# The decay factors of a long convolution's filters: exponentials on ScalarE instead of 32 loads

## The chip, the core and the metric

The kernel runs on one core of one Trainium2 chip. TensorE (PE) multiplies matrices into an accumulator memory, PSUM, of eight banks; VectorE (DVE) and ScalarE (ACT) work elementwise; GpSimd (POOL) and SyncE (SP) mostly start DMA transfers. Each engine works through its own list of instructions in the order in which they stand, and waits at an instruction until the others have signalled what it needs. The metric is the device time of one execution in microseconds, as the median of several runs.

## What is computed

One block of a diffusion backbone over 1024 latent tokens of width 1024, with 256 context tokens: a modulated norm and one wide input projection; then two token mixers side by side, a neighbourhood attention and a Hyena long convolution; their merge, and a gated feed-forward layer. The change touches the convolution's filters, which depend on no token. For two orders and two directions a small network of the time step gives 512 channels, and each is damped by an exponential decay:

```
t = jnp.linspace(0.0, 1.0, L)[:, None]
hid = jnp.sin(fr * (z @ w1 + b1));  hid = jnp.sin(fr * (hid @ w2 + b2))
h = (hid @ w3).reshape(L, 2, HY_ORDER, HY_WIDTH)
deltas = jnp.abs(jnp.linspace(min_decay, max_decay, HY_WIDTH))
decay = jnp.exp(-t * deltas)
return h * decay[:, None, None, :]
...
k2 = jnp.concatenate([h_fwd, jnp.zeros((1, C)), h_bwd[:0:-1]], axis=0)
y = irfft(rfft(u, n=2 * L) * rfft(k2, n=2 * L))[:L]
```

The decay depends on the time and the channel alone, so it is a constant. The backward filter is used in reversed time, and its first row is zero.

## The kernel before

Tokens or time steps lie on the 128 partitions. Products that need more than one pass of precision are made of three matmuls on a high and a low part of each operand (`split`: ACT casts the high part, `wh` or `oh`; DVE subtracts for the low one, `wl` or `ol`).

Around the change, from about 70 to 300 us, three streams of work are written by Python generators and merged by their planned weights; a scheduler then fixes the order of each engine's list when the program is built:

- `project`, the input projection: a chunk of 128 output columns takes 2 x 24 matmuls of 128x512 (`in_ps`, line 195), chunks of keys and values 24 of 128x256 on the context as well (`ctx_ps`). SP loads the weights (`wr`, line 181), ACT copies results out (`proj`, `projc`), PE turns some of them (`tm_ps`) and ACT copies those (`tm`).
- `filters`, with four groups: two halves `hf` of 256 channels times two orders `o`. I number them 1 to 4 in the order of the program. In a group, four steps of two time blocks each take for both directions `j`: four matmuls into two banks (`filt_ps`, line 363), and two multiplications by the decay tile on DVE (`fv`, line 370), which I call a pair. The decay tiles (`dec`, line 359) are loaded by SP, 128x512 each, from a table that the host computes; `bufs=2` gives them two buffers, so the tile of the next pair may only be loaded when the multiplication of this pair has read its buffer. The matmul results have five banks (`psf`) in common with the stream's other results. Then come DVE's sums and twiddles (lines 376 to 430), whose results `a` are the operands of eight DFTs on PE (`dft_ps`, lines 442 to 444). ACT copies the spectra out (`ks`), and SP writes them to memory (`spec`).
- `ada_rows`, the remaining modulation rows: DVE adds up 64 tiles of a weight (`wal`, loaded by SP into four buffers, line 887) times a column (`aacc`, lines 890 and 892); PE sums over partitions (`ar_ps`) and DVE adds the result (`arow`).

After the filters the same merging goes on with the convolutions, up to about 600 us, and then with attention; the merge and the feed-forward layer follow.

Of the kernel before, what the change touches and what calls it, by code (L numbers as in the profile page):

```python
# [10 lines left out]
F32 = mybir.dt.float32  # L11
F32R = mybir.dt.float32r
AF = mybir.ActivationFunctionType
ALU = mybir.AluOpType
# [4 lines left out]
P = 128  # L19
# [23 lines left out]
def _constants():  # L43

    f32 = np.float32
    out = {}
    n1 = np.arange(P)[:, None].astype(np.float64)
    k1 = np.arange(P)[None, :].astype(np.float64)
    fwd = np.zeros((4, P, 2, 3, P), f32)
    inv = np.zeros((4, P, 2, 3, P), f32)  # L50
    for ci, ks in enumerate(CLASSES):
        for j, kk in enumerate(ks):
            th = TWO_PI * np.mod(n1 * (16 * k1 + kk + 0.5), 2048.0) / 2048.0
            c, s = np.cos(th), np.sin(th)
            if j:
                s = -s
            fwd[ci, :, j, 0], fwd[ci, :, j, 1], fwd[ci, :, j, 2] = c, s, -s
            inv[ci, :, j, 0], inv[ci, :, j, 1], inv[ci, :, j, 2] = c.T, -s.T, s.T
    out["dft_f"], out["dft_i"] = fwd, inv

    L = T
    t = np.linspace(0.0, 1.0, L, dtype=f32)
    w = (f32(TWO_PI) * np.arange(L, dtype=f32)) / f32(L)
    bands = np.linspace(1e-4, 15, 16, dtype=f32)
    bw = bands[None, :] * w[:, None]
    z = np.concatenate([t[:, None], np.cos(bw.astype(np.float64)), np.sin(-bw.astype(np.float64))], 1).astype(f32)
    rev = (L - np.arange(L)) % L
    out["feat"] = np.ascontiguousarray(np.concatenate([z.T, z[rev].T], 0))
    lo, hi = math.log(1e-2) / 1.5, math.log(1e-2) / 0.3
    deltas = np.abs(np.linspace(lo, hi, 512, dtype=f32))  # L70
    dec = np.exp((-t[:, None] * deltas[None, :]).astype(np.float64)).astype(f32) * f32(2.0 ** -10)
    drev = dec[rev].copy()
    drev[0] = 0.0
    both = np.stack([dec, drev], 1).reshape(4, 2, P, 2, 2, 256)
    out["decay"] = np.ascontiguousarray(both.transpose(4, 0, 3, 2, 1, 5)).reshape(2, 4, 2, P, 512)

    tok = np.arange(T)
    rows, cols = (tok // 64).astype(f32), (tok % 64).astype(f32)
    invf = (f32(10000.0) ** (-np.arange(16, dtype=f32) / f32(16))).astype(f32)
    cs, sn = np.zeros((P, T), f32), np.zeros((P, T), f32)  # L80
    for p in range(P):
        d = p % 64
        ang = ((rows if d < 32 else cols) * invf[d % 16]).astype(f32).astype(np.float64)
        cs[p] = np.cos(ang)
        sn[p] = np.sin(ang) * (-1.0 if d % 32 < 16 else 1.0)
    out["rope"] = np.stack([cs, sn])

    return out
# [70 lines left out]
class Block:  # L159
# [43 lines left out]
    def setup(self, pool):  # L203
        nc, a = self.nc, self.a
        self.ident = pool.tile([P, P], F32, name="ident")
        make_identity(nc, self.ident)
        self.eps = pool.tile([P, 1], F32, name="eps")
        nc.vector.memset(self.eps, EPS)
        cc = pool.tile([P, 8, 2], F32, name="cc")
        nc.sync.dma_start(cc, a["cc"])  # L210
        self.cs = pool.tile([P, 48], F32, name="cs")
        nc.vector.memset(self.cs[:, 16:], 0.0)
        nc.scalar.activation(self.cs[:, 0:16], cc.rearrange("p k w -> p (k w)"), AF.Silu)
        self.ng = pool.tile([P, 2, 8], F32, name="ng")
        self.bcol = pool.tile([P, 2, 8], F32, name="bcol")
        self.cw = pool.tile([P, 12, 4], F32, name="cw")
        self.mod1 = pool.tile([P, 2, 2, 8], F32, name="mod1")
        self.mod2 = pool.tile([P, 2, 8], F32, name="mod2")

# [46 lines left out]
    def hidden(self, pool, wpool, mp, hid, w3, hT, hcT, psf):  # L266
        nc, a = self.nc, self.a
        xs = []
        ssq = pool.tile([P, 10], F32, name="ssq1")
        ps = psf.tile([P, 512], F32, tag="f", name="ada_ps")  # L270
# [19 lines left out]

        mlp = self.filter_hidden(mp, hid, psf)
        next(mlp)
        for n in ("ng", "bcol", "cw"):
            nc.scalar.dma_start(getattr(self, n), a[n])
        for k in range(8):
            w = pool.tile([P, 2048], F32, tag="wada", name="wada", bufs=3)
# [51 lines left out]
    def filters(self, pool, psf, hid, w3):  # L348

        nc, a = self.nc, self.a  # L350
        for hf in range(2):
            for o in range(2):
                v = [pool.tile([P, 4, 2, 256], F32, tag="v8", name="fv") for _ in range(2)]
                c0 = o * 512 + hf * 256
                for n2 in range(0, 8, 2):
                    dec, ps = [], []
                    for j in range(2):
                        dec.append(pool.tile([P, 512], F32, tag="dec", name="dec", bufs=2))
                        nc.sync.dma_start(dec[j], a["decay"][hf, n2 // 2, j])
                        ps.append(psf.tile([P, 512], F32, tag="f", name="filt_ps"))  # L360
                    for n in range(2):
                        for j in range(2):
# [4 lines left out]
                                self.tc.keep_in_program_order(mm)  # L367
                    for j in range(2):
                        i = n2 % 4
                        nc.vector.tensor_tensor(v[n2 // 4][:, i:i + 2, j, :], ps[j].rearrange("p (n c) -> p n c", n=2),  # L370
                                                dec[j].rearrange("p (n c) -> p n c", n=2), op=ALU.mult)
                    yield 1.3
                b = pool.tile([1, 256], F32, tag="hb", name="hb", bufs=1)
                nc.sync.dma_start(b, a["hbias"][0:1, o, hf, :])
# [1097 lines left out]
```

## Time and profile before

| what | value |
|---|---|
| runs, median | 1711.23 us (1708.59 to 1711.89, 3 runs) |
| profiled execution, span | 1711.4 us |
| PE busy | 1657.6 us, 97% |
| DVE busy | 1230.1 us, 72% |
| ACT busy | 662.6 us, 39% |
| DMA | 282.48 MB, mean 165 GB/s |
| decay loads | 32 of 256 KB, issued from 75.3 to 274.0 us |

The profile is of one execution. A row of a timeline gives start and length in microseconds, engine, line, operation, output and inputs by the program's names, their shapes, and, in brackets, how long the engine had been idle before and what ended that wait. Runs of like instructions are shown as one row with their number. A row that groups instructions by line gives their number, busy time, mean duration in nanoseconds, and the idle time just before them with its releasers. The "granted clock" is the share of full speed that TensorE's throttle gave.

### The profile page before, as it was taken

The page shows a single profiled execution, that of the slowest core. Times are in us where ns is not written, and L with a number is a line of the kernel's source. Part 1 is how long each engine was busy: PE and PEld are TensorE (multiplying, and loading weights), DVE is VectorE, ACT ScalarE, POOL GpSimd, SP SyncE. Part 2 cuts the span into 40 slices and gives each one's busy share as a digit, 9 for nine tenths or more (in the row PEclk, how much of TensorE's full clock was granted, in tenths as well). Part 3 has the DMA queues.
Part 4 walks back from the last instruction along what each step waited for, and adds up shares of the span by engine and source line. Part 5 has one row for each costly group of instructions (what it writes and reads, how often), then busy time and mean ns, then how long its engine had stood idle before and what let it go on. Part 6 is the DMA issues. An engine that isn't in the chain of part 4 may idle for free.

```text
span 1711.4 us, 22611 instructions
## 1 busy us (share of the span) xinstructions
PE 1657.6 (97%) x8124; PEld 1307.2 (76%) x8124; DVE 1230.1 (72%) x2076; ACT 662.6 (39%) x1141; POOL 153.3 (9%) x274
## 2 busy tenths in 40 slices
PE   6898999999999999999999999999999999999997
PEld 2676776777777778888787888888888888878886
DVE  3697586699995966465865967867865566479576
ACT  4621221312221224455654315733333333355455
POOL 0100211101010014020200000010101011000000
PEclk9999999999999999999999999999999999999999
DMA  9276854645553456344657524333423223395334
GB/s 364 103 255 199 266 173 158 215 139 187 167 201 137 160 187 186 126 148 131 197 174 245 187 65 160 124 124 117 160 99 110 94 99 109 105 383 177 98 120 154
DMA packets 114517, 282.48 MB, mean 165 GB/s; under 512 B 15840, under 2 KB 24676, under 8 KB 112102
## 3 DMA queue, kind: packets, MB, share of 16 engines
q1 hardware_dynamic: 94472, 219.99, 38.6%
q0 software_dynamic: 19280, 60.60, 10.5%
q8 instruction: 64, 1.05, 0.3%
q10 hardware_dynamic: 653, 0.44, 0.1%
q14 instruction: 48, 0.39, 0.1%
HBM read 213.60 MB, written 67.39 MB: 164 GB/s over the span
## 4 chain that ended last, share of the span: by engine, by line
PE 65%; issue 10%; DVE 4%; DMA 2%; ACT 1%; POOL 1%; SPq 0%; DVEq 0%; POOLq 0%; ACTq 0%
PE x_ps L1171 15%; PE in_ps L195 12%; PE z_ps L1171 7%; PE dx_ps L1340 6%; PE out_ps L1109 4%; PE dz_ps L1340 3%; PE hy_ps L195 2%; PE y_ps L1171 2%; PE dft_ps L442 2%; PE pt_ps L800 2%; PE pt_ps L786 2%; PE na_ps L195 2%; PE dy_ps L1340 1%; PE s_ps L766 1%; PE dft_ps L444 1%
## 5 line engine op out<-in xcount | busy, mean ns | idle before, releaser
L195 PE MATMUL in_ps<-hTh,wl 128*128 128x512 f32 x640 | 260.0, 407 | 0.9 <-ACT proj L614 0.5
L195 PE MATMUL in_ps<-hTl,wh 128*128 128x512 f32 x640 | 254.5, 398 | 0.4 <-DVE hTl L176 0.2
L195 PE MATMUL in_ps<-hTh,wh 128*128 128x512 f32 x640 | 253.9, 397 | 0.0
L195 PEld LDWEIGHTS in_ps<-hTh,wl 128*128 128x128 f32 x640 | 121.5, 190 | 32.2 <-issue 5.6
L195 PEld LDWEIGHTS in_ps<-hTl,wh 128*128 128x128 f32 x640 | 121.8, 190 | 27.1 <-DVE hTl L176 1.8
L195 PEld LDWEIGHTS in_ps<-hTh,wh 128*128 128x128 f32 x640 | 121.6, 190 | 26.9 <-issue 0.4
L175 ACT CAST wh<-wr 128x1024 fp32r<-128x1024 f32 (+1 forms) x56 | 51.9, 926 | 141.4 <-PE in_ps L195 110.0
L176 DVE TENSOR_TENSOR wl<-wr,wh 128x1024 fp32r<-128x1024 f32 (+1 forms) x56 | 59.8, 1067 | 63.2 <-ACT wh L175 63.1
L176 DVE TENSOR_TENSOR ol<-ws,oh 128x512 fp32r<-128x512 f32 x88 | 60.4, 688 | 50.6 <-ACT oh L175 50.3
L176 DVE TENSOR_TENSOR ol<-ar,oh 128x512 fp32r<-128x512 f32 x77 | 52.8, 687 | 47.7 <-ACT oh L175 47.7
L175 ACT CAST oh<-ar 128x512 fp32r<-128x512 f32 x77 | 47.9, 622 | 84.4 <-PE dx_ps L1340 33.1
L175 ACT CAST oh<-ws 128x512 fp32r<-128x512 f32 x88 | 54.7, 622 | 57.1 <-PE x_ps L1171 27.5
L442 PE MATMUL dft_ps<-a,matf 128*128 128x512 f32 x128 | 67.1, 606 | 5.0 <-DVE a L430 4.1
L775 ACT ACTIVATE pe<-pe,mx 128x640 f32<-128x640 f32 x64 | 52.6, 822 | 48.9 <-DVE mx L774 48.9
L1340 PE MATMUL dx_ps<-ol,oh 128*128 128x512 f32 x176 | 68.7, 390 | 1.7 <-DVE ol L176 1.7
L774 DVE CUSTOM_DVE_ANT_0 pe<-s_ps,bias 128x640 f32<-128x640 f32 x64 | 50.1, 820 | 28.1 <-PE s_ps L769 28.1
L1340 PE MATMUL dx_ps<-oh,ol 128*128 128x512 f32 x176 | 67.4, 390 | 1.9 <-DVE ol L176 1.9
L1340 PE MATMUL dx_ps<-oh 128*128 128x512 f32 x176 | 68.5, 389 | 0.0
L176 DVE TENSOR_TENSOR ol<-wr,oh 128x512 fp32r<-128x512 f32 x70 | 48.0, 688 | 22.3 <-ACT oh L175 22.2
L175 ACT CAST oh<-wr 128x512 fp32r<-128x512 f32 x70 | 43.3, 622 | 52.3 <-PE x_ps L1171 16.0
L890 DVE SCALAR_TENSOR_TENSOR aacc<-wal,cs,aacc 128x512 f32<-128x512 f32 x56 | 41.8, 747 | 23.1 <-DMA wal<-in_w_ada 22.5
L1111 DVE TENSOR_TENSOR x<-x,out_ps 128x512 f32<-128x512 f32 x64 | 42.6, 683 | 15.2 <-PE out_ps L1109 15.0
(394 smaller groups left out, 4193.7 us busy)
## 6 DMA issues: line engine op xcount, KB each, us to landing
wr<-in_w SPq DMA_DIRECT2D x52, 512.0 KB, 3.4
wr<-in_w_in SPq DMA_DIRECT2D x40, 512.0 KB, 4.2
ar<-g SPq DMA_DIRECT2D x77, 256.0 KB, 2.8
wal<-in_w_ada SPq DMA_DIRECT2D x64, 256.0 KB, 4.1
matf<-in_dft_f SPq DMA_DIRECT2D x32, 384.0 KB, 4.7
bias<-in_rpb SPq DMA_DIRECT2D x64, 192.0 KB, 3.7
g<-t POOLq DMA_DIRECT2D x47, 256.0 KB, 3.0
w<-in_w SPq DMA_DIRECT2D x44, 256.0 KB, 5.4
```

The costliest lines, as they stand in the source:

```text
L175: self.nc.scalar.copy(hi, src)
L176: self.nc.vector.tensor_sub(lo, src, hi.bitcast(F32))
L195: mm = nc.tensor.matmul(ps, ww[:, k * P:(k + 1) * P], xx[:, k, pos:pos + width], start=(i == 0), stop=(i == n - 1))
L442: nc.tensor.matmul(ps, m[:, 0], v.rearrange("p a b -> p (a b)"), start=True, stop=False)
L774: nc.vector.tensor_tensor_reduce(pe, ps[:, 256:896], bt, -1.0, 3e38, ALU.add, ALU.min, mx[:, 0:1])
L775: nc.scalar.activation(pe, pe, AF.Exp, bias=mx[:, 0:1], scale=-1.0, accum_out=mx[:, 1:2])
L786: pin(nc.tensor.transpose(pt[:, at:at + P], pe[:, c * P:(c + 1) * P], self.ident))
L890: nc.vector.scalar_tensor_tensor(acc, w, c, acc, op0=ALU.mult, op1=ALU.add)
L1109: nc.tensor.matmul(ps, gg[x][:, tk], ww[y][:, sl], start=(i == 0), stop=(i == n - 1))
L1111: nc.vector.tensor_add(x1[:, sl], x1[:, sl], ps)
L1171: mm = nc.tensor.matmul(ps, w[u][:, k * P:(k + 1) * P], x[v][:, k, :], start=(start and k == 0 and i == 0), stop=(stop and k == 3 and i == 2),
L1340: nc.tensor.matmul(ps[j], x[u][:, j * P:(j + 1) * P], w[v], start=(start and i == 0 and c == 0), stop=(stop and i == N - 1 and k == len(re ...
```

## The change

The table of decays is gone. The host gives two small arrays instead: `rates`, the decay rate of each channel, and `times`, for each time block and direction the negated time of each partition (with 1000 where the backward filter's first row has to vanish). `times` is loaded once, on ACT's queue, behind three other small loads; `rates` is loaded by SP once for each half, spread over the partitions. Each decay tile is made of two ACT instructions: the exponential of `rates` times the partition's column of `times`. It keeps its two buffers. The factor 2^-10, until now in the table, goes into the multiplication, which becomes an operation with two factors.

```diff
-    dec = np.exp((-t[:, None] * deltas[None, :]).astype(np.float64)).astype(f32) * f32(2.0 ** -10)
...
-    out["decay"] = np.ascontiguousarray(both.transpose(4, 0, 3, 2, 1, 5)).reshape(2, 4, 2, P, 512)
+    tr = t[rev].copy()
+    tr[0] = 1000.0
+    out["rates"] = np.ascontiguousarray(deltas.reshape(2, 1, 256))
+    out["times"] = np.ascontiguousarray(-np.stack([t, tr], -1).reshape(8, P, 2).transpose(1, 0, 2))
...
+        self.times = pool.tile([P, 8, 2], F32, name="times")
...
-        for n in ("ng", "bcol", "cw"):
+        for n in ("ng", "bcol", "cw", "times"):
             nc.scalar.dma_start(getattr(self, n), a[n])
...
         for hf in range(2):
+            rates = pool.tile([P, 256], F32, tag="rates", name="rates", bufs=1)
+            nc.sync.dma_start(rates, a["rates"][hf].broadcast_to((P, 256)))
             for o in range(2):
...
                         dec.append(pool.tile([P, 512], F32, tag="dec", name="dec", bufs=2))
-                        nc.sync.dma_start(dec[j], a["decay"][hf, n2 // 2, j])
+                        for n in range(2):
+                            nc.scalar.activation(dec[j][:, n * 256:(n + 1) * 256], rates, AF.Exp,
+                                                 scale=self.times[:, n2 + n, j:j + 1])
...
-                        nc.vector.tensor_tensor(v[n2 // 4][:, i:i + 2, j, :], ps[j].rearrange("p (n c) -> p n c", n=2),
-                                                dec[j].rearrange("p (n c) -> p n c", n=2), op=ALU.mult)
+                        nc.vector.scalar_tensor_tensor(
+                            v[n2 // 4][:, i:i + 2, j, :], ps[j].rearrange("p (n c) -> p n c", n=2), 2.0 ** -10,
+                            dec[j].rearrange("p (n c) -> p n c", n=2), op0=ALU.mult, op1=ALU.mult)
```

The scheduler sees other work, and so the lists of all engines change between the first filter group and the end of the fourth; from there on they are the same. Line numbers of the changed kernel are a few higher (the exponentials are line 362, the multiplications 374, the DFTs 447 to 449).

ACT's list at group 1, before:

```order
L175 CAST wh<-wr 128x1024
L634 COPY projc<-ctx_ps 128x256
L175 CAST wh<-wr 128x1024
L634 COPY projc<-ctx_ps 128x256
L594 COPY proj<-in_ps 128x512 x2
```

And the same place in the change:

```order
L174 CAST wh<-wr 128x1024
L639 COPY projc<-ctx_ps 128x256
L362 ACT_TABLE_LOAD
L362 ACTIVATE dec<-rates,times 128x256 x10
L174 CAST wh<-wr 128x1024
L362 ACTIVATE dec<-rates,times 128x256 x4
L639 COPY projc<-ctx_ps 128x256
L362 ACTIVATE dec<-rates,times 128x256 x5
L599 COPY proj<-in_ps 128x512
L362 ACTIVATE dec<-rates,times 128x256
L599 COPY proj<-in_ps 128x512
```

Of the group's 16 exponentials, ten stand ahead of the next weight's cast and six behind it; the last four of these twenty belong to group 2's first pair. In group 2, sixteen stand in a row behind the last `ks` copy.

DVE's list at group 2, before (the sums `aacc` of the modulation rows stand between the pairs):

```order
L890 SCALAR_TENSOR_TENSOR aacc<-wal,cs,aacc 128x512 x3
L370 TENSOR_TENSOR fv<-filt_ps,dec 128x2x256 x2
L900 TENSOR_TENSOR arow<-ar_ps,arow 64x256
L375 SCALAR_TENSOR_TENSOR fv<-hb,fv 1x256
L890 SCALAR_TENSOR_TENSOR aacc<-wal,cs,aacc 128x512 x2
L370 TENSOR_TENSOR fv<-filt_ps,dec 128x2x256 x2
L890 SCALAR_TENSOR_TENSOR aacc<-wal,cs,aacc 128x512
L892 TENSOR_SCALAR aacc<-wal,cs 128x512
L890 SCALAR_TENSOR_TENSOR aacc<-wal,cs,aacc 128x512
L370 TENSOR_TENSOR fv<-filt_ps,dec 128x2x256 x2
```

And in the change:

```order
L895 SCALAR_TENSOR_TENSOR aacc<-wal,cs,aacc 128x512 x3
L374 SCALAR_TENSOR_TENSOR fv<-filt_ps,dec 128x2x256 x2
L905 TENSOR_TENSOR arow<-ar_ps,arow 64x256
L380 SCALAR_TENSOR_TENSOR fv<-hb,fv 1x256
L374 SCALAR_TENSOR_TENSOR fv<-filt_ps,dec 128x2x256 x2
L897 TENSOR_SCALAR aacc<-wal,cs 128x512
L374 SCALAR_TENSOR_TENSOR fv<-filt_ps,dec 128x2x256
L895 SCALAR_TENSOR_TENSOR aacc<-wal,cs,aacc 128x512
L374 SCALAR_TENSOR_TENSOR fv<-filt_ps,dec 128x2x256 x2
L895 SCALAR_TENSOR_TENSOR aacc<-wal,cs,aacc 128x512
```

No sum stands between the first and the second pair any more. Behind the group's first two DFT operands, nine sums now stand ahead of the next weight's `wl` and the fifth operand, where four did.

PE's list at group 2, before (the matmuls of the filters among those of the projection):

```order
L363 MATMUL filt_ps<-fw_280,hid 128x256 x4
L897 MATMUL ar_ps<-aacc,ones 32x256 x2
L363 MATMUL filt_ps<-fw_280,hid 128x256 x9
L195 MATMUL in_ps<-hTh,wl 128x512
L195 MATMUL in_ps<-hTl,wh 128x512
L195 MATMUL in_ps<-hTh,wh 128x512
L195 MATMUL in_ps<-hTh,wl 128x512
L363 MATMUL filt_ps<-fw_280,hid 128x256 x3
L195 MATMUL in_ps<-hTl,wh 128x512
```

And in the change:

```order
L367 MATMUL filt_ps<-fw_281,hid 128x256 x4
L902 MATMUL ar_ps<-aacc,ones 32x256 x2
L367 MATMUL filt_ps<-fw_281,hid 128x256 x12
L194 MATMUL in_ps<-hTh,wl 128x512
L194 MATMUL in_ps<-hTl,wh 128x512
```

All sixteen filter matmuls now stand ahead of the projection's. Further on in both lists come 48 (before: 44 more) projection matmuls, 24 of the context, the next `ar_ps`, and then the group's first DFT: behind 37 more projection matmuls before, behind 16 in the change. In group 1 the first DFT stands ten projection matmuls earlier as well.

More of the change, by code (lines that the diff above doesn't have):

```diff
@@ L70, in _constants @@
     deltas = np.abs(np.linspace(lo, hi, 512, dtype=f32))
-    dec = np.exp((-t[:, None] * deltas[None, :]).astype(np.float64)).astype(f32) * f32(2.0 ** -10)
-    drev = dec[rev].copy()
-    drev[0] = 0.0
-    both = np.stack([dec, drev], 1).reshape(4, 2, P, 2, 2, 256)
-    out["decay"] = np.ascontiguousarray(both.transpose(4, 0, 3, 2, 1, 5)).reshape(2, 4, 2, P, 512)
+    tr = t[rev].copy()
+    tr[0] = 1000.0
+    out["rates"] = np.ascontiguousarray(deltas.reshape(2, 1, 256))
+    out["times"] = np.ascontiguousarray(-np.stack([t, tr], -1).reshape(8, P, 2).transpose(1, 0, 2))
     tok = np.arange(T)
```

## The prediction

> **What bounds the kernel now.** I read the page first, then busy time by stretch, then what each engine waited for between 66 and 305 us, where the filters are made, then the timelines of TensorE (PE) and VectorE (DVE) around each stall. Row one is the page's; the others are the view by stretch (length, busy time of PE, PEld, DVE, ACT and POOL, granted clock, DMA share, GB/s).
>
> ```profile
> PE 1657.6 (97%) x8124; PEld 1307.2 (76%) x8124; DVE 1230.1 (72%) x2076; ACT 662.6 (39%) x1141; POOL 153.3 (9%) x274
> 84.00:92.00 8.00, 5.74 (x20) 4.41 (x20) 5.03 (x8) 1.32 (x2) 0.58 (x1) 0.79 0.75 251
> 138.00:150.00 12.00, 7.79 (x22) 5.79 (x23) 5.43 (x9) 0.00 (x0) 0.00 (x0) 0.72 0.84 270
> 231.00:239.00 8.00, 6.07 (x17) 3.67 (x16) 6.81 (x13) 1.10 (x4) 2.56 (x4) 0.79 0.56 181
> 262.00:273.00 11.00, 7.73 (x22) 5.74 (x23) 6.31 (x10) 0.00 (x0) 0.08 (x1) 0.69 0.79 250
> 342.00:428.00 86.00, 85.85 (x358) 64.19 (x358) 83.11 (x146) 18.70 (x27) 6.55 (x9) 1.00 0.50 162
> 428.00:514.00 86.00, 86.00 (x363) 64.89 (x362) 79.53 (x142) 20.74 (x30) 7.67 (x11) 1.00 0.56 186
> ```
>
> PE is the bound: 97% of the span, and without a hole from 342 to 514. Time can only be won where PE stands idle or runs at a lower clock. Both happen in the four stretches above, one per filter group, and there the clock is granted for 0.79, 0.72, 0.79 and 0.69 of the time: (1 - share) x length gives 1.7, 3.4, 1.7 and 3.4 us lost. Now PE's stalls themselves, from its timeline (start, length, and in brackets the idle time before and what ended it):
>
> ```profile
> 79.86 1.20 PE L363 MATMUL filt_ps<-fw,hid 64*128 64x256 f32 x8 [0.46 <-DVE fv L370]
> 86.26 0.91 PE L363 MATMUL filt_ps<-fw,hid 64*128 64x256 f32 x5 [2.42 <-DVE fv L370]
> 134.75 2.00 PE L363 MATMUL filt_ps<-fw,hid 64*128 64x256 f32 x16 [0.70 <-ACT ks L389]
> 142.21 2.07 PE L363 MATMUL filt_ps<-fw,hid 64*128 64x256 f32 x6 [4.33 <-DVE fv L370]
> 184.74 1.13 PE L442 MATMUL dft_ps<-a,matf 128*128 128x512 f32 x2 [0.83 <-DVE a L430]
> 188.21 1.10 PE L442 MATMUL dft_ps<-a,matf 128*128 128x512 f32 x2 [0.55 <-DMA matf<-in_dft_f]
> 233.55 1.54 PE L442 MATMUL dft_ps<-a,matf 128*128 128x512 f32 x2 [1.93 <-DVE a L430]
> 265.27 1.23 PE L363 MATMUL filt_ps<-fw,hid 64*128 64x256 f32 x4 [3.48 <-DVE fv L370]
> ```
>
> PE waits for a bank of accumulator memory that DVE's multiply (`fv`) frees, or for a DFT operand (`a`) at the end of DVE's chain. What DVE waited for decides whether the change reaches a stall:
>
> ```profile
> 85.51 1.29 DVE L370 TENSOR_TENSOR fv<-filt_ps,dec 128x512 f32<-128x512 f32 x2 [3.49 <-DMA dec<-in_decay]
> 141.46 1.39 DVE L370 TENSOR_TENSOR fv<-filt_ps,dec 128x512 f32<-128x512 f32 x2 [3.67 <-DMA dec<-in_decay]
> 214.29 0.69 DVE L370 TENSOR_TENSOR fv<-filt_ps,dec 128x512 f32<-128x512 f32 x1 [3.59 <-DMA dec<-in_decay]
> 219.42 0.69 DVE L370 TENSOR_TENSOR fv<-filt_ps,dec 128x512 f32<-128x512 f32 x1 [0.97 <-DMA dec<-in_decay]
> 263.74 0.75 DVE L890 SCALAR_TENSOR_TENSOR aacc<-wal,cs,aacc 128x512 f32<-128x512 f32 x1 [4.86 <-DMA wal<-in_w_ada]
> DVE aacc L890 <- DMA wal<-in_w_ada: 22.5, 15, 4.9
> DVE fv L370 <- DMA dec<-in_decay: 20.3, 14, 3.7
> SPq L359 <- DVE fv L370: 15.6, 24, 2.6
> ```
>
> The stalls of groups 1, 2 and 3 go back to decay loads: two buffers, so a load starts only when the multiply before the last has read its buffer (the last row: SP's queue stood 15.6 us for that), and the next multiply waits out the transfer. The stall of group 4 doesn't: there DVE waited for an adaLN weight (`wal`). So 4.6 us hang on the loads in group 1 (0.46 + 2.42 + 1.7), 8.4 in group 2 (0.70 + 4.33 + 3.4), 3.6 in group 3 (1.93 + 1.7), and 6.9 in group 4 do not.
>
> **The change, part by part.** *Removed:* 32 loads of 256 KB and their 32 places in SP's queue. *Added:* two loads of `rates`, one of `times`, 64 exponentials of 128x256 and one table load on ScalarE (ACT). The exponentials' price is bounded by rows of ACT and DVE before (count | busy us, mean ns; the SP row gives min/median/max ns of an issue, the row of DMA issues the KB and us to landing, and the last two are from ACT's timeline):
>
> ```profile
> L634 ACT COPY projc<-ctx_ps 128x256 f32<-128x256 f32 x8 | 2.9, 366 | 0.0
> L262 ACT ACTIVATE htmp<-hT_ps,mod 128x256 f32<-128x256 f32 x4 | 2.2, 563 | 1.1 <-PE hT_ps L248 0.8 <-DVE hcTl L176 0.3
> L239 ACT ACT_TABLE_LOAD x2 | 2.6, 1283 | 0.0
> L359 SPq DMA_DIRECT2D dec<-in_decay x32: 327/328/432, 75.3 to 274.0; - x32
> L370 DVE TENSOR_TENSOR fv<-filt_ps,dec 128x512 f32<-128x512 f32 x32 | 21.4, 688 | 21.5 <-DMA dec<-in_decay 20.3 <-PE filt_ps L363 1.1
> L890 DVE SCALAR_TENSOR_TENSOR aacc<-wal,cs,aacc 128x512 f32<-128x512 f32 x56 | 41.8, 747 | 23.1 <-DMA wal<-in_w_ada 22.5
> wal<-in_w_ada SPq DMA_DIRECT2D x64, 256.0 KB, 4.1
> 84.60 1.04 ACT L175 CAST wh<-wr 128x1024 fp32r<-128x1024 f32 x1 [6.47 <-DMA wr<-in_w_in]
> 215.22 0.37 ACT L571 COPY tm<-tm_ps 128x256 f32<-128x256 f32 x1 [4.04 <-DMA vtok<-tm]
> ```
>
> A copy of that size takes 0.37, one with both a scale and a bias column 0.56; with one column I take 0.45: 64 x 0.45 + 1.3 = 30 us. ACT does 0 to 1.3 us of work in each of the four stretches above, so this is hidden as work; what can hurt is its place in ACT's queue. A pair of decay tiles now costs 4 x 0.45 = 1.8 us on ACT, half of which overlaps the other tile's multiply, instead of a wait of about 3.6. The multiply gets a second factor: 0.747 for 0.688, 32 x 0.06 = 1.9 us of DVE, inside DVE's idle time; without that cover it would be 1.9. `times` goes to ACT's queue at the start, some cycles of issue before work that waits for `x`; I cost it at nothing (bound: one issue, 0.33 to 0.43 on SP).
>
> *Group 1, 4.6 now.* The first multiply now stands behind two sums (`aacc`) whose `wal` must land, some 4 us after issue; I walk the third multiply, which frees PE's last bank, to about 84 us against 86.3 now. PE then waits about 0.3 + 0.8 + 0.4 = 1.5 us in three pieces; pieces of 0.83 and 0.55 at 184 to 188 cost no clock. Gain 3.1 (bounds 4.6, nothing left, and -1: PE also comes to the group's DFT ten projection matmuls earlier, where I find DVE only half a microsecond ahead).
>
> *Group 2, 8.4 now.* The 0.70 for ACT's `ks` copy stays, and some 0.4 at the banks. But a new wait arises. In the changed order the first DFT stands after 16 projection matmuls behind `ar_ps`, not 37. DVE's way from the third multiply to the DFT operand, from the rows of now:
>
> ```profile
> 150.84 0.69 DVE L370 TENSOR_TENSOR fv<-filt_ps,dec 128x512 f32<-128x512 f32 x1 [0.29 <-DMA dec<-in_decay]
> 151.56 1.23 DVE L378 TENSOR_TENSOR fx<-fv 128x1024 f32<-128x1024 f32 x1
> 160.57 1.23 DVE L176 TENSOR_TENSOR wl<-wr,wh 128x1024 fp32r<-128x1024 f32 x1 [0.91 <-ACT wh L175]
> 166.52 1.27 DVE L430 SCALAR_TENSOR_TENSOR a<-x,b 128x512 f32<-128x512 f32 x2
> 78.54 0.28 PE L195 MATMUL ctx_ps<-hcTh,wh 128*128 128x256 f32 x1
> 78.66 0.28 PE L195 MATMUL ctx_ps<-hcTh,wl 128*128 128x256 f32 x1
> 168.07 0.39 PE L195 MATMUL in_ps<-hTh,wh 128*128 128x512 f32 x1
> 168.29 0.39 PE L195 MATMUL in_ps<-hTh,wl 128*128 128x512 f32 x1
> ```
>
> From the sums' start (151.56) to the first operand's end (166.5 + 0.7) 15.6, less the 0.91 wait, plus a sum more and a small product less, 15.0; ahead of it five multiplies with their exponentials and four sums, 6.2: 21.2 us, up to 22 where a `wal` is late. PE's way: 48 + 16 projection matmuls at 0.23 (168.07 to 168.29), 24 context ones at 0.12 (78.54 to 78.66) and 1.3 for the rest: 18.9. PE waits 2.3 to 3.1; I take 2.8. A wait of 1.93 in group 3 was followed by a lower clock worth 1.7, so 1.7 more. Left: 0.7 + 0.4 + 2.8 + 1.7 = 5.6; gain 2.8 (bounds 8.4, and -2.4 if a `wal` comes 3.5 late: 6.3 of waiting, 3.4 of clock, 1.1).
>
> [...]
>
> *Group 3, 3.6 now.* Its multiplies waited for loads up to the last (219.42). Now the last pair's second tile stands on ACT behind a copy (`tm`) that ran at 215.2; I put the last multiply at 217.2, not 220.1, and one `wl` (1.2) now stands behind the DFT operand. Together 4 us earlier against a wait of 1.93: gone with its clock. Exponentials between ACT's `tm` copies, for whose bank PE waits, cost 0.5. Gain 3.1 (bounds 3.6 and 0).
>
> *Group 4:* `wal` stands as before and the DMA engines are 0.79 busy there with no decay in flight: 0. *The 0.83 and 0.55* at 184 to 188: three sums leave the place ahead of the late operand; 0.5 (0 to 1.4).
>
> Sum: 3.1 + 2.8 + 3.1 + 0.5 = 9.5. The profiled span is 1711.4, 0.2 above the median of the runs. 1711.2 - 9.5 = 1701.7: **1702**. It carries to the end, since PE has no holes from 342 to 514 to swallow it, and DVE, 83.11 of 86 busy there, comes as much earlier because its order is the same from group 4 on.
>
> **Rivals.** *All of it.* No new wait: 4.6 + 8.4 + 3.6 + 1.4 = 18.0, so 1693. For: no row shows ACT busy there. Against: PE's earlier DFT.
> *A wash.* Decays stand in ACT's queue behind a `CAST wh` that waits for its own load in group 1, and behind the `tm` copy in group 3, and come no earlier than the loads did: those 8.2 stay, group 2 gives its 2.8: 1708 to 1709. For: that cast now waits until 84.6. Against: the bank PE needs is freed by the third multiply, whose exponentials stand ahead of the cast.
> *Slower.* The sums take the loads' place: DVE now runs `aacc` in rows of three to nine ahead of multiplies and operands, and a late `wal` stops PE as it does in group 4 today, at 6.9 a place. In three places (group 1's multiply, group 2's first DFT, its fifth) 20.7, with the 1.6 that stay anyway, against 18.0 freed: +4.3, **1715.5**. With two it is still a gain; the third decides. For: 22.5 us of such waits now. Against: 8 MB less traffic in front of them.
>
> **How the numbers follow.** About 0.2% (3.4 us) can be told from no change: faster is below 1707.8, slower above 1714.7. The forecast with its own range of 1697 to 1707 has 0.52, all of it 0.13, a wash 0.22, slower 0.13. Faster 0.65, same 0.22, slower 0.13. The range 1694 to 1714 leaves out half of the first rival and most of the last.
>
> **What would show it.** No wait of DVE for a decay load, 64 exponentials near 0.45 us, one more table load; PE's waits at the filter matmuls of groups 1 and 2 below 1 us each; a new wait of 2 to 3 us at group 2's first DFT, with clock lost; no wait at group 3's DFT; group 4 as now, 3.5 and 3.4. Wrong if PE waits for ACT's exponentials by name, if exponentials take 0.6 or more, if group 4's stall moves, or if the clock's loss doesn't follow the stalls.

## The result, and the profile after

The changed kernel takes 1695.84 us in the median (1693.85 to 1698.15, 4 runs) against 1710.82 us before; the ratio is 0.992, with a 95% interval from 0.99 to 0.9939. That is 15.0 us less, where 9.5 were forecast. On a second chip, where both kernels ran again later, the medians are 1699.93 and 1710.01, which is 10.1 less. Its profiled execution has a span of 1691.6 us, and its own time was 1693.98.

First the page's row of PE, and the view by stretch of the changed kernel. The stretches are not all the same as before, because everything behind group 1 comes earlier.

```profile
PE 1645.8 (97%) x8124; PEld 1302.7 (77%) x8124; DVE 1229.1 (73%) x2076; ACT 689.6 (41%) x1206; POOL 153.3 (9%) x274
78.00:84.00 6.00, 4.79 (x34) 3.83 (x31) 4.67 (x7) 4.78 (x10) 3.12 (x7) 1.00 0.86 295
84.00:92.00 8.00, 8.00 (x37) 6.09 (x37) 7.13 (x12) 6.34 (x15) 0.58 (x1) 1.00 0.87 282
150.00:166.00 16.00, 14.26 (x60) 10.87 (x60) 15.22 (x25) 1.90 (x5) 0.96 (x2) 1.00 0.47 146
231.00:239.00 8.00, 8.00 (x38) 6.51 (x37) 3.92 (x8) 1.33 (x2) 0.00 (x0) 1.00 0.74 270
249.00:257.00 8.00, 5.79 (x21) 3.94 (x19) 6.72 (x11) 4.62 (x11) 0.00 (x0) 0.79 0.61 203
```

The granted clock is 1.00 from 30.6 to 252.4 us, and so in groups 1, 2 and 3; one half-clock window is left, in group 4 (0.50 from 252.45 to 255.87). PE's holes of more than half a microsecond, from its timeline between 78 and 256 us ("issue" as the releaser means that the profile shows nothing that PE waited for):

```profile
82.54 1.86 PE L367 MATMUL filt_ps<-fw,hid 64*128 64x256 f32 x8 [1.14 <-DVE fv L374]
125.62 1.10 PE L447 MATMUL dft_ps<-a,matf 128*128 128x512 f32 x2 [0.58 <-issue]
154.94 1.10 PE L447 MATMUL dft_ps<-a,matf 128*128 128x512 f32 x2 [1.74 <-issue]
179.28 1.10 PE L447 MATMUL dft_ps<-a,matf 128*128 128x512 f32 x2 [1.43 <-DMA matf<-in_dft_f]
251.78 1.45 PE L367 MATMUL filt_ps<-fw,hid 64*128 64x256 f32 x6 [2.21 <-DVE fv L374]
```

The wait at 154.94 is the new one that was forecast, at group 2's first DFT; DVE's operand for it is done at about 154.9. The new instructions, and what DVE and ACT waited for from 66 to 305 us (us in total, times, longest):

```profile
L362 ACT ACTIVATE dec<-rates,times 128x256 f32<-128x256 f32 x64 | 27.7, 499 | 16.6 <-DVE fv L374 11.5 <-DMA rates<-in_rates 4.7
L362 ACT ACT_TABLE_LOAD x1 | 1.3, 1283 | 0.7 <-DMA rates<-in_rates 0.7
L374 DVE SCALAR_TENSOR_TENSOR fv<-filt_ps,dec 128x512 f32<-128x512 f32 x32 | 21.1, 684 | 3.8 <-PE filt_ps L367 2.0 <-ACT dec L362 1.5
DVE aacc L895 <- DMA wal<-in_w_ada: 16.9, 15, 4.0
```

DVE's 20.3 us of waiting for decays have become 1.5, and no hole of PE is put down to ACT's exponentials.

One profile of each kernel turned out not to be enough. I took a second one of each later, on one other chip, and the table sets all four beside the forecast. Each entry is PE's idle time plus 1.7 us for each half-clock window that followed (3.41 us at a granted 0.50); "forecast" is what the prediction left at that place.

| place | before | before, again | forecast | changed | changed, again |
|---|---|---|---|---|---|
| group 1, multiplications | 4.6 | 2.0 | 1.5 | 1.1 | 2.8 |
| 107 (`ar_ps`) and group 1's last DFTs | 0.6 | 1.0 | 0.6 | 0.6 | 0.8 |
| group 2 | 8.4 | 6.0 | 5.6 | 2.1 | 2.3 |
| 179 to 188, DFT operand and table | 1.4 | 1.9 | 0.9 | 1.4 | 4.2 |
| group 3's DFT | 3.6 | 2.0 | 0.5 | 0.4 | 0.4 |
| group 4 | 6.9 | 4.1 | 6.9 | 3.9 | 2.1 |
| sum | 25.5 | 17.0 | 16.0 | 9.5 | 12.6 |

The pairs differ by 16.0 and by 4.4, and by 10.2 in the mean. The holes of the kernel before again and of the changed kernel again, in this order:

```profile
85.41 1.13 PE L363 MATMUL filt_ps<-fw,hid 64*128 64x256 f32 x6 [1.56 <-DVE fv L370]
138.96 2.02 PE L363 MATMUL filt_ps<-fw,hid 64*128 64x256 f32 x6 [3.71 <-DVE fv L370]
229.65 1.12 PE L442 MATMUL dft_ps<-a,matf 128*128 128x512 f32 x2 [1.96 <-DVE a L430]
258.32 1.92 PE L363 MATMUL filt_ps<-fw,hid 64*128 64x256 f32 x6 [2.40 <-DVE fv L370]
```

```profile
82.28 1.86 PE L367 MATMUL filt_ps<-fw,hid 64*128 64x256 f32 x8 [1.07 <-DVE fv L374]
156.67 1.10 PE L447 MATMUL dft_ps<-a,matf 128*128 128x512 f32 x2 [2.01 <-issue]
182.44 1.10 PE L447 MATMUL dft_ps<-a,matf 128*128 128x512 f32 x2 [2.50 <-DMA matf<-in_dft_f]
256.57 1.13 PE L367 MATMUL filt_ps<-fw,hid 64*128 64x256 f32 x6 [2.11 <-DVE fv L374]
```

The holes come again at the same places. What changes from one execution to the next is their length, and more than that the number of half-clock windows behind them: six in the first profile of the kernel before, two in the second.

A second part of the gain lies where the change touches nothing. Between the last norm and the feed-forward layer's last products PE runs without a hole, and yet the two kernels differ (before, then changed; the number behind PE's busy time counts its matmuls):

```profile
1200.00:1300.00 100.00, 100.00 (x438) 82.07 (x437) 74.28 (x117) 34.73 (x59) 12.94 (x24) 1.00 0.35 121
1300.00:1400.00 100.00, 100.00 (x438) 82.07 (x437) 59.14 (x92) 39.87 (x70) 8.11 (x16) 1.00 0.30 104
```

```profile
1200.00:1300.00 100.00, 100.00 (x443) 82.81 (x442) 69.24 (x108) 37.61 (x65) 10.28 (x19) 1.00 0.31 106
1300.00:1400.00 100.00, 100.00 (x443) 82.81 (x442) 62.36 (x97) 38.55 (x67) 11.33 (x21) 1.00 0.32 109
```

438 matmuls in 100 us against 443. The stage from 1071.1 to 1502.3 us takes 431.2 before and 427.5 after: 3.7 us less, with the same order of instructions.

### The profile page after: what moved, and what is told of

Its sections match the earlier page's. It is cut to its first block, busy times and chain, and to the rows that moved or that the text cites. A ratio compares the mean times of both kernels' runs of the same rounds, so it can differ in the third digit from the quotient of the medians.

```text
span 1691.6 us, 22631 instructions
## 1 busy us (share of the span) xinstructions
PE 1645.8 (97%) x8124; PEld 1302.7 (77%) x8124; DVE 1229.1 (73%) x2076; ACT 689.6 (41%) x1206; POOL 153.3 (9%) x274
## 4 chain that ended last, share of the span: by engine, by line
PE 68%; issue 11%; DVE 5%; DMA 3%; ACT 1%; POOL 1%; SPq 0%; DVEq 0%; POOLq 0%; ACTq 0%
PE x_ps L1176 15%; PE in_ps L194 13%; PE z_ps L1176 7%; PE dx_ps L1345 6%; PE out_ps L1114 4%; PE dz_ps L1345 3%; PE dft_ps L447 2%; PE hy_ps L194 2%; PE y_ps L1176 2%; PE pt_ps L805 2%; PE pt_ps L791 2%; PE na_ps L194 2%; PE dy_ps L1345 1%; PE dft_ps L448 1%; PE dft_ps L449 1%
## 5 line engine op out<-in xcount | busy, mean ns | idle before, releaser
L175 DVE TENSOR_TENSOR ol<-ws,oh 128x512 fp32r<-128x512 f32 x88 | 60.4, 688 | 49.1 <-ACT oh L174 49.0
L174 ACT CAST oh<-wr 128x512 fp32r<-128x512 f32 x70 | 43.3, 621 | 51.3 <-PE x_ps L1176 15.5
L1116 DVE TENSOR_TENSOR x<-x,out_ps 128x512 f32<-128x512 f32 x64 | 42.7, 684 | 16.9 <-PE out_ps L1114 16.7
L895 DVE SCALAR_TENSOR_TENSOR aacc<-wal,cs,aacc 128x512 f32<-128x512 f32 x56 | 41.8, 746 | 17.5 <-DMA wal<-in_w_ada 16.9
```

Of the source, the lines that this page charges most:

```text
L174: self.nc.scalar.copy(hi, src)
L175: self.nc.vector.tensor_sub(lo, src, hi.bitcast(F32))
L895: nc.vector.scalar_tensor_tensor(acc, w, c, acc, op0=ALU.mult, op1=ALU.add)
L1116: nc.vector.tensor_add(x1[:, sl], x1[:, sl], ps)
```

## The experiments

My theory was that the multiplications' wait for a decay load, itself made by the two buffers, is what the change removes. The rivals were that the gain comes from 8 MB less traffic or from a shorter queue on SP, or that the holes are only moved. Runs of the kernel before stand beside each experiment on its chip: 1709.49 in the median for the first four, 1710.01 for the next four, 1708.79 for the three after, 1708.25 for the last.

**The loads as dead weight.**

```diff
+                        nc.sync.dma_start(self.idle.pop(), a["decay"][hf, n2 // 2, j])
                         for n in range(2):
                             nc.scalar.activation(dec[j][:, n * 256:(n + 1) * 256], rates, AF.Exp,
```

> The changed kernel, with the 32 loads of the decay table put back as dead loads: SP starts each at the place of its pair, but the data goes to a scratch array in device memory that nothing reads. The order on PE, DVE and ACT is that of the change; SP has 32 more issues and the DMA engines 8 MB more to read and write. If the gain came from the multiplications' wait for a load, the time stays at the change's, 1695 to 1698 us, with PE's holes within 0.5 us of the change's. If it came from the freed queue or the freed traffic, the weights of ada_rows come late again, and the time goes back to 1702 to 1709.

Measured: 1698.8 us, 0.8 above the range for no loss, ratio 0.9931 (0.9908 to 0.9955). The changed kernel itself, on the second chip, has 0.9936 (0.9918 to 0.9954). So the traffic and the issues in SP's queue cost nothing that can be measured, though the intervals leave room for some 4 us. These loads wait for no buffer, so the 15.6 us for which SP stood at the old ones stay away here; the fourth experiment bears on that. The holes are not all within 0.5 us of the change's: group 2's first DFT waits 3.27 here and the DFT table 1.95. But DVE waits for `wal` as long as in the change (17.2 us against 16.9).

**The exponentials as dead work in the kernel before.**

```diff
                         nc.sync.dma_start(dec[j], a["decay"][hf, n2 // 2, j])
+                        idle = pool.tile([P, 256], F32, tag="idle", name="idle", bufs=1)
+                        for n in range(2):
+                            nc.scalar.activation(idle, hid[:, 0:256], AF.Exp, scale=self.times[:, n2 + n, 0:1])
```

> The kernel before, with its loads, and beside them the 64 exponentials on ACT as dead work: 128x256 each with a column as scale, one in the place of each half tile, into a scratch tile that nothing reads. Some ten instructions of PE and DVE change places. If the exponentials are covered on ACT, as I forecast, the time stays at 1711 (1708 to 1713). If their place in ACT's list hurts (the casts of the weights or the ks copies come late), PE's holes at the groups grow by about 1 us each and the time rises by 3 to 6.

Measured: 1707.06 us, ratio 0.9984 (0.9967 to 1.0001). The time does not rise: 34 us of new work on ACT (32.6 of exponentials and a table load of 1.3) are covered. All 64 exponentials run between 76.8 and 119.4 us, because they wait for nothing, so this prices the work but not its places in groups 2 to 4. The holes shift all the same: one of 2.37 us at 102 is new, and group 2's is 2.52 where it was 4.33. (The time lies just below the range expected. This kernel holds the tile `times`, and so has the faster feed-forward stage of the last experiment, 443 matmuls from 1100 to 1200 us; the ratio there, 0.9985, is the same.)

**The spectra written from ACT's queue.**

```diff
-                            nc.sync.dma_start(self.spec[o][hf][ci - 1][j], k)
+                            nc.scalar.dma_start(self.spec[o][hf][ci - 1][j], k)
```

> The changed kernel, with the 32 writes of the spectra (spec) started by ACT right behind its ks copy, and no longer by SP. The order on PE is that of the change, on DVE three instructions change places. My theory of group 4's stall after the result: SP stood at a spec write that waits for ACT's ks, behind it the load of the weight (wal) that DVE's sum and so the first multiplication wait for. Then the hole of 2.2 us before group 4's filter matmuls goes below 0.5 with its half-clock window, and the time is 3 to 4 below the change's, 1692. The rival, that the stall is one of traffic (the load itself is slow): the hole stays at 2 or more and the time at 1696.

Measured: 1699.82 us, ratio 0.9931 (0.9908 to 0.9954), and this theory fell. SP now starts the weight's load at 247.82 without standing at a spectrum, and DVE and PE wait as before (the rows are SP's, DVE's, PE's, and the stretch, whose last two numbers are the DMA share and GB/s):

```profile
247.82 1.90 SPq L892 DMA_DIRECT2D wal<-in_w_ada  x3
252.98 1.54 DVE L895 SCALAR_TENSOR_TENSOR aacc<-wal,cs,aacc 128x512 f32<-128x512 f32 x2 [2.82 <-DMA wal<-in_w_ada]
255.29 1.13 PE L367 MATMUL filt_ps<-fw,hid 64*128 64x256 f32 x6 [2.50 <-DVE fv L374]
244.00:253.00 9.00, 8.79 (x46) 5.45 (x44) 5.92 (x12) 3.17 (x6) 3.25 (x5) 1.00 0.89 300
```

Three loads are issued between 247.8 and 249.7, and the sums behind them start at 252.98; meanwhile the DMA engines are 0.89 busy with a projection weight, spectra, tables and token tiles. That fits the rival, a load that is slow in the traffic of its stretch, but for the time, which the rival had at 1696; what helps against it, the buffers show below.

**The loads without the wait.**

```diff
-                        dec.append(pool.tile([P, 512], F32, tag="dec", name="dec", bufs=2))
-                        nc.sync.dma_start(dec[j], a["decay"][hf, n2 // 2, j])
+                        dec.append(v[n2 // 4][:, n2 % 4:n2 % 4 + 2, j, :])
+                        nc.sync.dma_start(dec[j], a["decay"][hf, n2 // 2, j].rearrange("p (n c) -> p n c", n=2))
```

> The kernel before, with its 32 loads, but each goes straight into the place of its product in fv, which the multiplication overwrites, so that no decay tile has to be freed first and the loads of a group may run ahead. No exponentials, and 4 KB per partition less memory. If the wait for the two buffers was what the stalls of groups 1 to 3 hung on, most of the gain comes without the exponentials: 1695 to 1702, and DVE's wait for decay loads falls from 20 us to below 6. If a load's traffic and its place in the queue were the matter, DVE still waits 12 us or more and the time stays above 1706.

Measured: 1703.19 us, ratio 0.9962 (0.9945 to 0.998). DVE's wait for the loads has gone:

```profile
DVE fv L370 <- DMA fv<-in_decay: 4.4, 2, 4.0
DVE aacc L890 <- DMA wal<-in_w_ada: 21.2, 10, 4.5
```

The holes of groups 1 and 2 at the multiplications sum to 2.5 us, and group 3's DFT doesn't wait, without one exponential. So the wait for a buffer was the cause there. SP still stands for 15.0 us in this kernel, until the tile `fx` is free, so SP's standing alone doesn't cost the time. Without the 0.0015 that the last experiment gives to the tiles' addresses, the change's 0.9936 would be 0.9951, inside this kernel's interval: the wait alone can account for the rest of the gain. The time is a little above the range I had written, since new holes of 2 us appear at 109 (behind a late projection weight) and at 181, each with a half-clock window behind it, and group 4 keeps 3.3.

**Both kernels once more.** No edit.

> The changed kernel once more, on the chip of these runs. If the holes of the first profile are the change's own, they come again: 1.1 in group 1, 1.7 at group 2's first DFT, 1.4 at the DFT's table (matf), 2.2 in group 4, each within 0.4. If they are chance, at least two of them move by more than 0.7 and the time spreads by more than 4 us over its runs; the median should be 1694 to 1700 in both cases.

> The kernel before once more, one profile. If group 4's stall (3.5 of idle time and two half-clock windows, 6.9) belongs to the kernel before, it comes again at 3.0 or more; if the 3.0 us that the change won there were chance, it comes at 2.0 to 2.6 with one window. The stalls of groups 1 and 2 on decay loads should come again at 2.4 and 4.3, within 0.7.

Measured: changed 1699.93 us, ratio 0.9936 (0.9918 to 0.9954); before, the profiled run, 1704.28, in a span of 1702.1. Their rows are shown above. The changed kernel's holes are its own, but for the DFT table's, which grew from 1.43 to 2.50; its runs spread over 4.7 us. In the kernel before, group 2's stall came again within 0.7 us, but group 1's did not (1.56 for 2.42). Group 4's stall there came at 2.40 with one half window, not at 3.48 with two. So the 3.0 us that the first pair of profiles shows as won in group 4 may be chance of the execution. But all profiles with four `wal` buffers together lean against chance alone: where the products use loaded decays the hole is 3.48, 2.40, 2.35 (dead exponentials), 3.30 (loads without the wait) and 3.44 (sixty-four bytes), and where they use exponentials 2.21, 2.11, 2.09 (dead loads), 2.50 (spectra) and 2.53 (exponentials in place). Whether the change shortens this hole, and how, stays open: in the first profile no decay load starts between 220.2 and 265.3 us, and the hole ends at 265.3.

**The exponentials in place of the product, and two more buffers for `wal`.**

```diff
-                        dec.append(pool.tile([P, 512], F32, tag="dec", name="dec", bufs=2))
+                        dec.append(v[n2 // 4][:, n2 % 4:n2 % 4 + 2, j, :])
...
-                            nc.scalar.activation(dec[j][:, n * 256:(n + 1) * 256], rates, AF.Exp,
+                            nc.scalar.activation(dec[j][:, n], rates, AF.Exp,
...
-                        w = pool.tile([P, 512], F32, tag="wal2", name="wal", bufs=4)
+                        w = pool.tile([P, 512], F32, tag="wal2", name="wal", bufs=6)
```

The first of the two kernels has the first two edits only.

> The changed kernel, with the exponentials written straight into the place of their product in fv, and no decay tile: ACT need not wait for a multiplication and may run a group ahead. ACT's 11.5 us of waiting for the multiplications should be gone. If the multiplications still waited for ACT (the trace shows 1.5 us), the time falls by 1 to 2 us; if they wait for sums and their weights, which I expect, it stays at the change's within 2 us, with holes of 1 us in group 1 and 2 us in group 4.

> As the in-place exponentials, with the 4 KB that they free given to two more buffers for the weights of ada_rows (wal, six for four). The order on PE is the same, five DVE instructions change places. If what is left in groups 1 and 4 are sums that wait for a late weight, DVE's wait for wal falls from 17 us to below 8, group 4's hole goes below 1 and the time falls by 3 to 5, to 1691 to 1694. If the loads are late by the traffic of their own stretch and not by their issue, the hole stays at 2 and the time with it.

Measured: in place alone 1696.11 us, ratio 0.9923 (0.9902 to 0.9943), beside 0.9936 of the change: the intervals overlap, though the median is 3.8 us below the change's on this chip, where I expected 2 at most. With six buffers 1686.37 us (1686.0 to 1688.6), ratio 0.986 (0.9839 to 0.9882), better than I expected. DVE's wait for `wal`, 15.5 us with four buffers, is

```profile
DVE aacc L895 <- DMA wal<-in_w_ada: 3.5, 3, 2.8
```

and from 70 to 300 us no half-clock window is left, and PE stands idle for 3.6 us in all, 1.11 of it still at group 1's multiplications. So most of what remained after the change were sums with a late weight, and they were late because only four could be on their way. (The two profiles account for 4.9 of the 9.7 us between the medians, since PE stands idle for 8.4 us with four buffers; that profile is of its kernel's fastest run.)

**The same buffers with loads.**

```diff
-                        w = pool.tile([P, 512], F32, tag="wal2", name="wal", bufs=4)
+                        w = pool.tile([P, 512], F32, tag="wal2", name="wal", bufs=6)
```

on the loads without the wait, and the exponentials with six buffers again.

> The kernel before, with its 32 loads going straight into the place of their product, and the 4 KB that this frees given to two more buffers for the weights of ada_rows (six for four). No exponentials. If the exponentials are needed only because they take loads out of a crowded stretch, group 4's hole stays at 2 or more and the time is 1699 to 1704. If buffers were all that was missing, it comes to within 3 us of the in-place exponentials with six buffers, 1686 to 1690.

> The in-place exponentials with six buffers for the weights of ada_rows, a second time and on the same chip as the loads with six buffers: 1684 to 1690, no hole of PE over 1.2 us from 66 to 300 us, and no half-clock window there.

Measured: loads 1694.94 us, ratio 0.9921 (0.9901 to 0.9941); exponentials 1687.98 us, ratio 0.9885 (0.9861 to 0.991). Group 4's hole is gone in both; the largest one with exponentials is 1.23 us, where 1.2 was the bound expected. Neither theory's number for the loads was met: loads in place with six buffers give as much as the change, and the exponentials 7.0 us more. PE's idle time from 60 to 310 us is 8.2 us with loads and 4.4 with exponentials, which is 3.8 of them. Only the kernel with exponentials holds `times`, and the last experiment puts 2.6 us on that by its ratio; together these would be 6.4 of the 7.0.

**A price for the clock.** A kernel of its own: bursts of matmuls, and between two bursts DVE works for a chosen time on a tile that the next burst reads (left out: the 64 to 76 matmuls into `ps`).

```python
for i, n in enumerate(WIDTHS):
    ...
    nc.vector.tensor_scalar(col, ps[:, 511:512], 0.0, 0.5, op0=mult, op1=add)
    nc.vector.tensor_scalar_mul(g[:, 0:n], x[:, 0:n], col)
```

> A kernel of its own that leaves out all of the block's computation: 56 bursts of 64 to 76 matmuls of 128x512 (about 15 us each), and between two of them a gap of PE that a DVE operation of chosen width makes, from about 0.9 to 3.7 us. It measures the term that failed in my sum, the clock's price of a hole. In the profiles so far the half clock comes in pieces of 3.41 us on one grid, so my theory is that PE's idle time within one such window decides, whatever the gap's length: windows with 1.9 us or more of it are followed by a half window, those with 1.4 or less are not, and a gap of 2 to 3 us costs clock or not according to where it falls on the grid. The rival: the gap's length decides, with one threshold between 1.7 and 1.9 us, and its place doesn't matter.

Measured: 55 gaps between bursts, of 0.64 to 2.06 us, and five half-clock windows between them, each of 3.41 us. Longer gaps did not come about, though up to 3.7 us was expected. Two gaps of nearly one length, by windows of the grid (length, PE busy; the granted clock is the third number from the right):

```profile
114.20:117.62 3.42, 1.52 (x8) 1.32 (x8) 1.68 (x2) 0.00 (x0) 0.00 (x0) 1.00 0.00 0
117.62:121.03 3.41, 3.41 (x10) 2.63 (x9) 0.00 (x0) 0.00 (x0) 0.00 (x0) 0.50 0.00 0
216.60:220.02 3.42, 3.04 (x14) 2.18 (x12) 0.31 (x2) 0.00 (x0) 0.00 (x0) 1.00 0.00 0
220.02:223.43 3.41, 1.86 (x9) 1.58 (x10) 1.40 (x1) 0.00 (x0) 0.00 (x0) 1.00 0.02 5
223.43:226.84 3.41, 3.41 (x17) 2.81 (x16) 0.00 (x0) 0.00 (x0) 0.00 (x0) 1.00 0.00 0
```

The gap of 1.90 lies within one window, PE is busy there for 1.52 of 3.42, and the next window runs at half clock. The gap of 1.93 lies across a boundary, no window has more than 1.55 us of it, and nothing follows. Over all windows between bursts: up to 1.77 us idle none is followed by a half window; from 1.80 on, five of six are (1.80, 1.83, 1.86, 1.90, 1.97; not a second one of 1.86). So in these bursts idle time within a window of the grid decides, not the gap's length: gaps of 1.90 to 2.03 us that lie across a boundary cost nothing.

The block's own profiles agree on the grid, and not on the bound of 1.8. In the kernel before, the stretches at half clock start at 87.36, 141.97, 234.13 and 264.85 us, that is 16, 27 and 9 times 3.41 apart, and last 3.41 or twice that. The hole of 3.27 us in the kernel with dead loads lies across a boundary, 1.62 and 1.66 us of idle time in its two windows, and costs no clock. But in the second profile of the changed kernel a window with 1.04 us idle is followed by half clock:

```profile
81.31:84.72 3.41, 2.37 (x12) 1.50 (x14) 3.41 (x7) 3.06 (x9) 0.36 (x1) 1.00 1.01 360
84.72:88.13 3.41, 3.41 (x11) 2.30 (x10) 2.21 (x5) 1.59 (x4) 0.00 (x0) 0.50 0.92 290
```

So are windows with 1.07, 1.42 and 1.67 (dead loads), 1.63 and 1.76 (dead exponentials), and 1.43 and 1.41 (six buffers, with loads and with exponentials), while windows with 1.80 and 1.85 in the second profile of the kernel before are not. In all those followed by half clock PE also runs matmuls on 64 of the 128 rows or 128x128 transposes, which the bursts don't have. That alone doesn't decide either: at the place of the 1.42 the kernel with the spectra on ACT's queue has 1.4 us idle too, and keeps its clock.

**Sixty-four bytes.**

```diff
-        self.cw = pool.tile([P, 12, 4], F32, name="cw")
+        self.cw = pool.tile([P, 12, 4], F32, name="cw"); self.pad = pool.tile([P, 8, 2], F32, name="times")
```

> The kernel before, with nothing but an unused tile of 64 bytes per partition, where the change puts times among the constants; every later tile lies 64 bytes higher, and no engine's order changes. In the profiles so far the feed-forward stage, which the change doesn't touch, has 438 or 439 matmuls per 100 us in the three kernels without times (before, in-place loads with four and with six buffers), and 442 or 443 in all that have it, the dead exponentials too. If the tiles' addresses set that pace, this kernel has 442 or 443 from 1100 to 1400 us and runs 3 to 5 us below the kernel before (ratio 0.997 to 0.998), with the stalls of groups 1 to 4 as before. If the pace comes from anything else that the change does, it has 438 and the ratio is 1.

Measured: 1706.08 us, ratio 0.9985 (0.9972 to 0.9998), 2.2 us in the medians, with stalls like those before (2.09, 3.96, 2.13 and 3.44 in the four groups). The feed-forward stage:

```profile
1200.00:1300.00 100.00, 100.00 (x443) 82.84 (x442) 74.37 (x117) 35.05 (x60) 13.49 (x25) 1.00 0.37 126
1300.00:1400.00 100.00, 100.00 (x443) 82.84 (x442) 59.11 (x91) 40.34 (x70) 8.07 (x15) 1.00 0.30 104
```

An unused tile that moves all later tiles by 64 bytes gives the changed kernel's pace, though less time than the 3 to 5 us expected. 442 or 443 stand in every kernel here that has `times`, and 438 or 439 in all that have neither it nor this tile.

## Why the prediction was right, and where not

The direction and the mechanism were right; the time lies in the range, just below the forecast's own (1697 to 1707), between it and the rival that had 1693. But the 15.0 us are not the forecast's 9.5 with every term a little larger. They are about 10 from the holes (16.0 and 4.4 in two pairs of profiles), for which the sum had 9.5, and about 3 from the addresses of the tiles, which stood in no step: 3.7 by the stage's length, 2.2 by the padded kernel's median and 2.6 by its ratio. The rest is within what the runs spread. That the holes' mean stands so near to 9.5 is in part luck, because the terms miss in both directions: by the means of the table group 1 gave 1.3 where 3.1 was put, group 2 5.0 for 2.8, group 3 2.4 for 3.1, group 4 2.5 for 0, and the table at 179 to 188 lost 1.2 where 0.5 was to be won.

- *What bounds the kernel.* Right: PE, and in groups 1 to 3 the decay loads' wait for a buffer. Taking the wait away and keeping the loads gives 0.9962; putting the loads back without the wait takes nothing from the change that can be measured (0.9931).
- *The exponentials.* Right: 499 ns in the mean, between the bounds of 0.37 and 0.56; 27.7 us and one table load of 1.283, where 30 us were taken. In a row they overlap: ten take 4.37 us (from 131.73), where one alone takes 0.51. The second factor cost nothing: 684 ns a multiplication against 688; the row of `aacc` that I took for it was the wrong neighbour.
- *Group 1.* Right in the mechanism: left 1.1 in one piece, and 1.1 with a half window in the second profile; 1.5 was forecast. That PE would come early to the group's DFT showed as 0.6 and 0.8.
- *Group 2.* The new wait came where it was put, but at 1.74 and 2.01, below the 2.3 to 3.1 that the walk gave. DVE's way, from the third multiplication to the operand, was forecast well:

```profile
132.70 1.45 DVE L374 SCALAR_TENSOR_TENSOR fv<-filt_ps,dec 128x512 f32<-128x512 f32 x2
154.16 1.28 DVE L435 SCALAR_TENSOR_TENSOR a<-x,b 128x512 f32<-128x512 f32 x2
```

  The first operand is done at 154.16 + 0.7, 22.2 us after 132.70, where 21.2 to 22 were forecast. PE's way, from 132.70 to 153.20, took 20.5 and not 18.9: 64 and 24 projection matmuls are 17.6 of it, and the term "1.3 for the rest" was mis-sized at 2.9, mostly the filters' own matmuls.
- *The clock's price there.* This is the step that failed: "1.7 more", because a wait of 1.93 had lost the clock in group 3. The waits of 1.74 and 2.01 lost none; the windows that hold most of them have 1.47 and 1.74 us of idle time, below the 1.8 that the bursts gave. In group 3 of the kernel before, the 1.93 lay within one window (230.72 to 234.13 us); in its second profile 1.96 was cut, 1.85 was in one, and no half window followed. A price of 1.7 was taken for sure, and a hole of this size pays it or not: by its place on a grid that lay differently in the two profiles of the changed kernel (half windows start at 252.45 us in one and at 84.72 in the other, 49.1 windows apart), and by something more that these runs don't settle, since windows with 1.04 to 1.76 us idle paid it elsewhere in the block.
- *Group 3.* Right: 3.1 forecast, 3.2 (and 1.6 by the second pair) measured; its DFT doesn't wait, and 0.43 is lost at a `tm` copy, where 0.5 was put.
- *Group 4.* The 6.9 "as now" was wrong as a number: it was one execution's draw of a hole that is 2.4 or 3.5 us in the two profiles of the kernel before, with one or two half windows behind it. Whether the 0 was right stays open: with four buffers the hole is 2.35 to 3.48 in the five profiles whose products use loaded decays, and 2.09 to 2.53 in the five where they use exponentials. Its cause, a late weight, was read rightly, and six buffers remove it.
- *The table at 179 to 188.* Half a microsecond of gain was forecast; 0 and a loss of 2.3 came. PE waits there for the DFT's table by name in all four profiles (0.55 and 1.08 before, 1.43 and 2.50 in the change), and I had counted sums ahead of the operand, not the table's load.
- *The rivals.* The slower one, sums in the loads' place, didn't come about: DVE's wait for `wal` fell from 22.5 to 16.9 us. What speaks against it is not the lighter traffic, as I had written, since the dead loads bring that back and the wait stays 17.2.
- *Its own signs of being wrong.* Two of them came: group 4's stall moved, and the clock's loss didn't follow the wait in group 2. PE's waits at the filter matmuls of group 1 were 1.14 and 1.07, a little above the 1 us given.

What stays open: why windows with as little as 1.04 us idle were followed by half clock in the block. PE's work in them is in part matmuls on 64 of the 128 rows or 128x128 transposes, but no run tests whether those count for less. Nor is it shown whether group 4's hole is shorter by the change. And which operand's address makes the pace of the feed-forward stage was not tried.

## What to carry to other kernels

Where a load waits for its buffer and the bound engine, through others, for the load, look at the wait first: here it was the cost, and not the load. A tile that is written straight into the place of its result needs no buffer at all, and the memory it frees can go to the next late load. That second step was worth about as much as the change itself here (1686.37 and 1687.98 us, ratios 0.986 and 0.9885). Before a gain is booked to a mechanism, take a second profile of the same kernel, and look at a stage that the edit doesn't touch.

## What the hardware showed that I had not expected

The clock was halved, to a granted 0.50, in windows of 3.41 us; in the kernel before the halved stretches start 16, 27 and 9 such windows apart. In the bursts a window with 1.80 us or more of idle time was followed by one at half clock in five cases of six, which costs 1.7 us, and a window with up to 1.77 in none; gaps of 1.90 to 2.03 us cut by a boundary cost nothing. In the block 1.8 us was no safe bound: eight windows with 1.04 to 1.76 us idle paid as well. The kernel before, with holes of 2 to 4 us, varied: it ranged from 1701.88 to 1717.52 us in 24 runs on one chip, and its two profiles differ by 9.3 us in span, 8.5 of it in the holes and windows of the table. Beside 11 runs of it that spread over 11.4 and 11 that spread over 11.0 us, the kernel with six buffers stayed within 2.6 (four runs) and 6.7 us (five). And the place of the tiles in memory, moved by 64 bytes, changed the pace of the feed-forward stage's matmuls, which run without a hole, by 1.1% (438 against 443 in 100 us).
